# Softmax on negated scores, two scalings of probabilities in place of four, later weight splits and an earlier read of gate sums in a two-layer decoder trunk

## The chip, the core and the metric

The kernel runs on one core of a Trainium2 chip. The core has five engines with a queue each, which work side by side and wait for one another by semaphores: TensorE (PE, with PEld for its weight loads), VectorE (DVE), ScalarE (ACT), GpSimd (POOL) and SyncE (SP), which here only issues DMAs. ACT issues a few DMAs too. The metric is the time of one execution on the device, in microseconds.

## What is computed

A trunk of two layers over 256 tokens of width 1024, all in float32. A layer is a half step of SwiGLU, a mixer, and another half step of SwiGLU; one RMS norm closes the trunk.

```python
for l in range(DEPTH):                     # 2
    x = x + 0.5 * swiglu(rms_norm(x, norm_ffn1[l]), w_ffn1_gate[l], w_ffn1_up[l], w_ffn1_down[l])
    x = x + hybrid_mixer(rms_norm(x, norm_mix[l]), ...)
    x = x + 0.5 * swiglu(rms_norm(x, norm_ffn2[l]), w_ffn2_gate[l], w_ffn2_up[l], w_ffn2_down[l])
return rms_norm(x, norm_final)

def swiglu(x, w_gate, w_up, w_down):       # d_ff 2816
    return (jax.nn.silu(x @ w_gate) * (x @ w_up)) @ w_down

def masked_softmax(s, valid):
    s = jnp.where(valid, s.astype(jnp.float32), NEG)
    m = jnp.max(s, axis=-1, keepdims=True)
    p = jnp.where(valid, jnp.exp(s - m), 0.0)
    return p / jnp.maximum(jnp.sum(p, axis=-1, keepdims=True), 1.0)
```

The mixer projects to queries, keys, values and gates and has 8 NSA heads in two groups (three branches: compressed keys, selected blocks, window) and 8 MoBA heads. At 256 tokens the selected blocks, the window and the MoBA block each cover all earlier tokens, so each head's scores are two blocks of 128 queries against 128 or 256 keys, masked causally. The NSA branches are weighted by gates, and a product with `w_out` closes the mixer.

## The kernel before

**Precision and splits.** Every weight block (128 x 1024, 512 KB, 322 of them in a fixed list) comes by a DMA on SP into one of 5 raw buffers. ACT rounds it to a high part (`whi`, L260), DVE subtracts to get a low part (`wlo`, L290), and TensorE multiplies high by high, high by low and low by high. There are 7 buffer pairs for split blocks. A block is split when a pair is free; `pump` keeps `st.reserve` pairs free, so a larger reserve means later splits. A raw buffer comes free, and the next load starts, when its low part is made.

**Half steps** (`ffn`). In turn of j (22 blocks of 128 hidden units) TensorE makes a gate and an up product (`wide`, L594 and L596: 512 columns with the high part, 256 with the low one, eight times) into PSUM banks: psB and psB for even j, psC and psD for odd. `read(j)` adds the two halves of a bank: ACT copies one (L680), DVE adds the other (L681). Then POOL, ACT and DVE form silu(gate) x up (`finish`), and `down` multiplies it into four banks psA. Where a half step starts behind another stage, its first two j run together (`gu_two`): four blocks, with the last part of the normed input still on its way. The next gate block needs the psB bank back, and so the sums of j = 0.

**Mixer.** `feature_one` makes each feature block with 24 matmuls (L565 to L567); between them stand the attention steps of earlier blocks: scores (`nsa_s`, L1101 and L1103), softmax, `normalize` (scaling by 1/sum and gate, on POOL), `transpose_p` (three transposes a half into a psA bank, L1074, copied out by ACT, L1076), products with the values (`pv`, L1084 and L1086, then the compressed branch, L1123). A softmax of an NSA head has two halves, r = 0 and 1 (selected and window branch); that of a MoBA head has one. For each half DVE adds the mask to the scores, multiplies by `rs8` (1/8 times the norm) and keeps the maximum (L1046 for the 256-wide block, L1047 for the 128-wide one); one instruction negates the maxima (L1049), and ACT makes the exponentials with that bias (L1051, L1052). New queries and keys pass `rope_begin` (ACT copies them raw, L820, and issues two DMAs that swap rows, L821 and L822) and `rope_end` (two POOL products, L826 and L827), then `stack_q` (casts on ACT, L834 and L835, and DVE, L836 and L837). Then come the MoBA values (`m_v`, L1181 to L1183) and the output product (L572 to L574, in `steps`), with the MoBA heads' steps in between.

**Order.** The program names each instruction's engine; the order on each engine is made by a scheduler that runs a model of the engines over the whole program. `tc.issue_after(i)` makes it place an instruction behind i. The stream of splits uses this by `st.behind`: what stands there for "A" or "V" is the instruction behind which ACT's or DVE's part of the following splits must come. The order is fixed when the program is built; on the chip every engine works through its own list.

```python
def queue(self, eng):
    return self.tc.issue_after(self.behind[eng]) if eng in self.behind else nullcontext()
```

Of the kernel before, what the change touches and what calls it, by code (L numbers as in the profile page):

```python
# [21 lines left out]
F32 = mybir.dt.float32  # L22
# [3 lines left out]
AF = mybir.ActivationFunctionType  # L26
OP = mybir.AluOpType
AX = mybir.AxisListType

D, S, L, DH = 1024, 256, 2, 64  # L30
# [287 lines left out]
def trunk(ctx, tc, xin, wst, w1st, gains, glast, cst, small, out, phases=PHASES, n_raw=5, n_hl=7):  # L318
    nc = tc.nc
    V, A, G, T = nc.vector, nc.scalar, nc.gpsimd, nc.tensor  # L320
# [3 lines left out]
    mp = ctx.enter_context(tc.tile_pool(name="mix", bufs=1))  # L324
# [319 lines left out]
    def ffn(pi, name, l):  # L644
# [31 lines left out]
        def read(j):  # L676

            s = S_[j] = mp.tile([128, 2, S], F32, name="hs", tag="PT", bufs=5)
            for i, o in enumerate(pend.pop(j)):
                A.copy(s[:, i], o[:, S:])  # L680
                V.tensor_add(s[:, i], s[:, i], o[:, :S])  # L681

        def finish(j):
            n = 0 if j == NJ - 1 else 1
# [119 lines left out]
    def mixer(pi, l):  # L804
# [95 lines left out]
        rotk = rawk[:, 2:4]  # L900
        rs = state["rs"]
        rs8 = mp.tile([128, 2], F32, name="rs8", bufs=2)
        nrs = mp.tile([128, 2], F32, name="nrs", bufs=2)
        G.tensor_scalar(rs8, rs, DH ** -0.5, None, op0=OP.mult)
        A.activation(warm, rs8[:, 0:1], AF.Exp, scale=0.0)
        G.tensor_scalar(nrs, rs, -1.0, None, op0=OP.mult)
# [130 lines left out]

        def softmax(key, s1, s0, nb, gates):

            P = mp.tile([128, 3, 2, 128], F32, name="P", tag="P", bufs=3)[:, :, :nb]  # L1040
            m = mp.tile([128, 2, nb], F32, name=f"mx{nb}", bufs=3)
            nm = mp.tile([128, 2, nb], F32, name=f"nm{nb}", bufs=3)
            sm = mp.tile([128, 2, nb], F32, name=f"sm{nb}", bufs=3)
            mk = m1.rearrange("p (k t) -> p k t", k=2)
            for r in range(nb):
                V.tensor_tensor_reduce(P[:, 0:2, r], s1[:, :, r], mk, rs8[:, 1:2], -3e38, OP.add, OP.max, m[:, 0, r:r + 1])  # L1046
                read = V.tensor_tensor_reduce(P[:, 2, r], s0[:, r], m0, rs8[:, 0:1], -3e38, OP.add, OP.max,  # L1047
                                              m[:, 1, r:r + 1]).ins
            V.tensor_scalar(nm, m, -1.0, None, op0=OP.mult)  # L1049
            for r in range(nb):  # L1050
                A.activation(P[:, 0:2, r], P[:, 0:2, r], AF.Exp, bias=nm[:, 0, r:r + 1], accum_out=sm[:, 0, r:r + 1])  # L1051
                e = A.activation(P[:, 2, r], P[:, 2, r], AF.Exp, bias=nm[:, 1, r:r + 1], accum_out=sm[:, 1, r:r + 1]).ins  # L1052
            if gates is not None:
                st.behind["A"] = e
            PR[key] = (P, sm, nb, gates)
            return read

        def normalize(key):
            P, sm, nb, gates = PR[key]
            V.reciprocal(sm, sm)  # L1060
            if gates is None:
                V.tensor_scalar(sm, sm, 1.0, None, op0=OP.min)
            else:
                V.scalar_tensor_tensor(sm, sm, 1.0, gates, op0=OP.min, op1=OP.mult)
            for r in range(nb):
                G.tensor_mul(P[:, 0:2, r], P[:, 0:2, r], sm[:, 0, r:r + 1, None].to_broadcast([128, 2, 128]))
                G.tensor_mul(P[:, 2, r], P[:, 2, r], sm[:, 1, r:r + 1].to_broadcast([128, 128]))

        def transpose_p(key, tag):
            P, _, nb, _ = PR.pop(key)  # L1070
# [167 lines left out]
        normalize(5)  # L1238
        m_end()
        nsa_s(6)  # L1240
        st.reserve = 2
        m_feat("mq", 2)
        nsa_pv(1)
        nsa_t(4)
# [62 lines left out]
        nsa_t(6)  # L1307
        normalize(("m", 0))
        moba_s(1)
        st.reserve = 1  # L1310
        st.behind.clear()
        m_v(1)
        nsa_t(7)
# [12 lines left out]
                 (moba_s, 7), (part, 3, 0), (normalize, ("m", 6)), (moba_pv, 2), (part, 3, 1), (moba_t, 6), (part, 4, 0),  # L1326
                 (normalize, ("m", 7)), (moba_t, 7), (part, 4, 1), (moba_pv, 3)]
        for f, *args in steps:
            if args == [4, 0]:
                st.reserve = 0  # L1330
            with tc.issue_after(last):
                last = f(*args) or last
        st.reserve = 1
# [71 lines left out]
```

## Time and profile before

| | before |
|---|---|
| median of 3 runs, us | 1021.62 (1019.35 to 1098.41) |
| profiled execution: its own time, us | 1018.07 |
| its span, first to last instruction, us | 1016.3 |
| busy, us: PE / PEld / DVE / ACT / POOL | 996.7 / 861.8 / 698.2 / 592.6 / 323.0 |
| mean granted TensorE clock | 0.997 |
| read from memory, MB | 182.04 |

About 1.8 us of the profiled execution's time lie outside its span. The stages of the span, in us: half step 0 to 200, first mixer 200 to 330, half steps 330 to 700, second mixer 700 to 830, last half step to the end. A wait is shown as the idle time of an engine ahead of an instruction, with what ended it. Only idle time on the engine that bounds the kernel costs time by itself. An engine's queue of DMA issues is named ACTq or SPq.

### The profile page before, as it was taken

The page shows a single profiled execution, that of the slowest core. Times are in us where ns is not written, and L with a number is a line of the kernel's source. Part 1 is how long each engine was busy: PE and PEld are TensorE (multiplying, and loading weights), DVE is VectorE, ACT ScalarE, POOL GpSimd, SP SyncE. Part 2 cuts the span into 40 slices and gives each one's busy share as a digit, 9 for nine tenths or more (in the row PEclk, how much of TensorE's full clock was granted, in tenths as well). Part 3 has the DMA queues.
Part 4 walks back from the last instruction along what each step waited for, and adds up shares of the span by engine and source line. Part 5 has one row for each costly group of instructions (what it writes and reads, how often), then busy time and mean ns, then how long its engine had stood idle before and what let it go on. Part 6 is the DMA issues. An engine that isn't in the chain of part 4 may idle for free.

```text
span 1016.3 us, 16192 instructions
## 1 busy us (share of the span) xinstructions
PE 996.7 (98%) x5873; PEld 861.8 (85%) x5873; DVE 698.2 (69%) x1195; ACT 592.6 (58%) x1137; POOL 323.0 (32%) x412
## 2 busy tenths in 40 slices
PE   9999999999899999999999999999999999999997
PEld 7888888899778888888888888889987788888885
DVE  6876566689984866666676656666899757666664
ACT  6755555557864855555575555456578756555552
POOL 2322122136751322222242222131477313222220
PEclk9999999999999999999999999999999999999999
DMA  8786776354452666666557677863436427666631
GB/s 275 249 292 198 266 251 214 105 171 149 130 166 84 213 205 193 195 188 189 164 186 207 188 232 231 280 189 125 158 110 185 132 84 252 198 212 187 189 123 42
DMA packets 52848, 188.21 MB, mean 185 GB/s; under 512 B 6368, under 2 KB 6752, under 8 KB 51616
## 3 DMA queue, kind: packets, MB, share of 16 engines
q1 hardware_dynamic: 49680, 182.17, 56.5%
q10 hardware_dynamic: 3088, 5.01, 1.8%
q8 instruction: 46, 0.75, 0.3%
q14 instruction: 34, 0.28, 0.1%
HBM read 182.04 MB, written 1.05 MB: 180 GB/s over the span
## 4 chain that ended last, share of the span: by engine, by line
PE 91%; DVE 4%; ACT 2%; issue 1%; POOL 1%; DMA 1%; ACTq 0%; POOLq 0%; DVEq 0%
PE psB L594 16%; PE psA L572 9%; PE psA L574 9%; PE psA L573 9%; PE psB L596 8%; PE psC L594 8%; PE psD L594 8%; PE psD L596 4%; PE psC L596 4%; PE psA L565 2%; PE psA L566 2%; PE psA L567 2%; PE psA L407 1%; PE psD L1084 1%; DVE wlo L290 1%
## 5 line engine op out<-in xcount | busy, mean ns | idle before, releaser
L290 DVE TENSOR_TENSOR wlo<-wraw,whi 128x1024 fp32r<-128x1024 f32 x325 | 411.1, 1272 | 208.7 <-ACT whi L260 208.3
L260 ACT CAST whi<-wraw 128x1024 fp32r<-128x1024 f32 (+1 forms) x326 | 337.7, 1044 | 276.3 <-issue 172.1
L594 PE MATMUL psB<-x,whi 128*128 128x512 f32 x688 | 242.4, 393 | 1.1 <-DVE hs L681 1.1
L689 POOL TENSOR_TENSOR hs<-hs,rbc 128x256 f32<-128x256 f32 x88 | 76.5, 871 | 400.7 <-DVE hs L681 366.5
L596 PE MATMUL psB<-x,wlo 128*128 128x256 f32 x688 | 192.6, 280 | 0.0
L594 PEld LDWEIGHTS psB<-x,whi 128*128 128x128 f32 x688 | 129.2, 188 | 30.0 <-DVE hs L681 1.9
L574 PE MATMUL psA<-wlo,hp 128*128 128x512 f32 (+1 forms) x356 | 137.6, 387 | 0.0
L573 PE MATMUL psA<-whi,hp 128*128 128x512 f32 (+1 forms) x356 | 137.5, 387 | 0.0
L572 PE MATMUL psA<-whi,hp 128*128 128x512 f32 (+1 forms) x356 | 137.0, 388 | 0.5 <-DVE X L470 0.5
L596 PEld LDWEIGHTS psB<-x,wlo 128*128 128x128 f32 x688 | 129.4, 188 | 1.4
L691 POOL TENSOR_TENSOR hs<-hs,rbc 128x256 f32<-128x256 f32 x88 | 101.8, 1160 | 72.2 <-ACT hs L690 72.0
L594 PE MATMUL psC<-x,whi 128*128 128x512 f32 x344 | 122.0, 392 | 0.0
L594 PE MATMUL psD<-x,whi 128*128 128x512 f32 x344 | 121.7, 391 | 0.0
L596 PE MATMUL psC<-x,wlo 128*128 128x256 f32 x344 | 96.2, 280 | 0.0
L596 PE MATMUL psD<-x,wlo 128*128 128x256 f32 x344 | 96.2, 280 | 0.0
L572 PEld LDWEIGHTS psA<-whi,hp 128*128 128x128 f32 x356 | 66.8, 188 | 14.3 <-DVE X L470 0.7
L574 PEld LDWEIGHTS psA<-wlo,hp 128*128 128x128 f32 x356 | 66.8, 188 | 13.7
L573 PEld LDWEIGHTS psA<-whi,hp 128*128 128x128 f32 x356 | 66.9, 188 | 12.2
L594 PEld LDWEIGHTS psD<-x,whi 128*128 128x128 f32 x344 | 64.6, 188 | 14.3
L594 PEld LDWEIGHTS psC<-x,whi 128*128 128x128 f32 x344 | 64.6, 188 | 14.1
L565 PE MATMUL psA<-x,whi 128*128 128x256 f32 x256 | 73.0, 285 | 0.0
L567 PE MATMUL psA<-x,wlo 128*128 128x256 f32 x256 | 72.3, 282 | 0.0
(245 smaller groups left out, 1599.8 us busy)
## 6 DMA issues: line engine op xcount, KB each, us to landing
wraw<-in_w SPq DMA_DIRECT2D x318, 512.0 KB, 4.3
W1a<-in_w SPq DMA_DIRECT2D x4, 1024.0 KB, 6.2
W1mixn<-in_w SPq DMA_DIRECT2D x2, 1024.0 KB, 6.4
W1late<-in_w SPq DMA_DIRECT2D x2, 1024.0 KB, 5.9
KM<-KM ACTq DMA_DIRECT2D x8, 256.0 KB, 3.8
wraw<-in_w SPq DMA_DIRECT2D x4, 420.0 KB, 3.1
wraw<-in_w SPq DMA_DIRECT2D x4, 256.0 KB, 4.8
X<-in_small SPq DMA_DIRECT2D x1, 1024.0 KB, 7.3
```

The source lines that it names most:

```text
L260: self.last_hi = self.nc.scalar.copy(hi[:, a:b], raw[:, a:b]).ins
L290: eng.tensor_sub(lo[:, :c], raw[:, :c], hi[:, :c].bitcast(F32))
L565: T.matmul(o, hi, xh, start=first, stop=False, skip_group_check=True)
L566: T.matmul(o, hi, xl, start=False, stop=False, skip_group_check=True)
L567: return T.matmul(o, lo, xh, start=False, stop=last, skip_group_check=True).ins
L572: T.matmul(o, parts[:, 0, c], hi, start=first, stop=False, skip_group_check=True)
L573: T.matmul(o, parts[:, 1, c], hi, start=False, stop=False, skip_group_check=True)
L574: return T.matmul(o, parts[:, 0, c], lo, start=False, stop=last, skip_group_check=True).ins
L594: T.matmul(o, blk128(hi, k), x.rearrange("p a t -> p (a t)"), start=k == 0, stop=k == KT - 1, skip_group_check=True)
L596: last = T.matmul(o[:, S:], blk128(lo, k), x[:, 0], start=False, stop=k == KT - 1, skip_group_check=True).ins
L689: G.tensor_mul(g, g, state["rbc"])
L691: G.tensor_mul(g, g, state["rbc5"])
```

## The change

Four things are changed.

1. Softmax: DVE multiplies scores plus mask by a negated factor (`nrs8`, a new tile of two values made on POOL) and keeps the minimum, which is the negated maximum. The instruction that negated is gone; ACT's exponentials take `scale=-1.0`.
2. `normalize`: one scaling for the 128-wide blocks of all halves, then one for the 256-wide ones, in place of two for each half.
3. `st.reserve` stays at 3 through the second part of the attention and the MoBA values. It goes to 2, 1 and 0 in the output product, ahead of its blocks 0, 2 and 4.
4. In `read(0)` of a half step other than the first, the second of DVE's two adds is put in `st.behind["V"]`: low parts of blocks that are split from then on come behind it on DVE.

```diff
             for i, o in enumerate(pend.pop(j)):
                 A.copy(s[:, i], o[:, S:])
-                V.tensor_add(s[:, i], s[:, i], o[:, :S])
+                add = V.tensor_add(s[:, i], s[:, i], o[:, :S]).ins
+            if j == 0 and pi > 0:
+                st.behind["V"] = add
...
+        nrs8 = mp.tile([128, 2], F32, name="nrs8", bufs=2)
         nrs = mp.tile([128, 2], F32, name="nrs", bufs=2)
+        G.tensor_scalar(nrs8, rs, -DH ** -0.5, None, op0=OP.mult)
...
-            m = mp.tile([128, 2, nb], F32, name=f"mx{nb}", bufs=3)
...
             for r in range(nb):
-                V.tensor_tensor_reduce(P[:, 0:2, r], s1[:, :, r], mk, rs8[:, 1:2], -3e38, OP.add, OP.max, m[:, 0, r:r + 1])
-                read = V.tensor_tensor_reduce(P[:, 2, r], s0[:, r], m0, rs8[:, 0:1], -3e38, OP.add, OP.max,
-                                              m[:, 1, r:r + 1]).ins
-            V.tensor_scalar(nm, m, -1.0, None, op0=OP.mult)
+                V.tensor_tensor_reduce(P[:, 0:2, r], s1[:, :, r], mk, nrs8[:, 1:2], 3e38, OP.add, OP.min,
+                                       nm[:, 0, r:r + 1])
+                read = V.tensor_tensor_reduce(P[:, 2, r], s0[:, r], m0, nrs8[:, 0:1], 3e38, OP.add, OP.min,
+                                              nm[:, 1, r:r + 1]).ins
             for r in range(nb):
-                A.activation(P[:, 0:2, r], P[:, 0:2, r], AF.Exp, bias=nm[:, 0, r:r + 1], accum_out=sm[:, 0, r:r + 1])
-                e = A.activation(P[:, 2, r], P[:, 2, r], AF.Exp, bias=nm[:, 1, r:r + 1], accum_out=sm[:, 1, r:r + 1]).ins
+                A.activation(P[:, 0:2, r], P[:, 0:2, r], AF.Exp, scale=-1.0, bias=nm[:, 0, r:r + 1],
+                             accum_out=sm[:, 0, r:r + 1])
+                e = A.activation(P[:, 2, r], P[:, 2, r], AF.Exp, scale=-1.0, bias=nm[:, 1, r:r + 1],
+                                 accum_out=sm[:, 1, r:r + 1]).ins
...
-            for r in range(nb):
-                G.tensor_mul(P[:, 0:2, r], P[:, 0:2, r], sm[:, 0, r:r + 1, None].to_broadcast([128, 2, 128]))
-                G.tensor_mul(P[:, 2, r], P[:, 2, r], sm[:, 1, r:r + 1].to_broadcast([128, 128]))
+            G.tensor_mul(P[:, 2], P[:, 2], sm[:, 1, :, None].to_broadcast([128, nb, 128]))
+            G.tensor_mul(P[:, 0:2], P[:, 0:2], sm[:, None, 0, :, None].to_broadcast([128, 2, nb, 128]))
...
         nsa_s(6)
-        st.reserve = 2
         m_feat("mq", 2)
...
         moba_s(1)
-        st.reserve = 1
         st.behind.clear()
...
-            if args == [4, 0]:
-                st.reserve = 0
+            if f is part and args[0] in (0, 2, 4) and args[1] == 0:
+                st.reserve = 2 - args[0] // 2
```

The scheduler makes a new order of the mixers and of the starts of the half steps from this. Three places follow. Line numbers of the rows after the change are those of the changed program, a few higher.

**DVE, start of the second half step of layer 1.** `x` is the normed input's low part, `wlo` a block's low part, `hs` a gate or up sum. Before:

```order
L389 SCALAR_TENSOR_TENSOR x_3575<-psA,g,x_3575 128x256 x4
L290 TENSOR_TENSOR wlo<-wraw,whi 128x1024 x4
L681 TENSOR_TENSOR hs<-hs,psB 128x256
L290 TENSOR_TENSOR wlo<-wraw,whi 128x1024
L681 TENSOR_TENSOR hs<-hs,psB 128x256
L681 TENSOR_TENSOR hs<-hs,psC 128x256
```

and after:

```order
L389 SCALAR_TENSOR_TENSOR x_3529<-psA,g,x_3529 128x256 x4
L681 TENSOR_TENSOR hs<-hs,psB 128x256 x2
L290 TENSOR_TENSOR wlo<-wraw,whi 128x1024 x3
L681 TENSOR_TENSOR hs<-hs,psC 128x256
L290 TENSOR_TENSOR wlo<-wraw,whi 128x1024 x2
L681 TENSOR_TENSOR hs<-hs,psD 128x256
```

Both sums of j = 0 now come ahead of all low parts, where four and then one stood ahead of them. The same has happened at the start of both half steps of layer 2. TensorE's list at this place, behind the last block of `gu_two` (psD), is after the change:

```order
L596 MATMUL psD<-x_3529,wlo 128x256
L594 MATMUL psB<-x_3529,whi 128x512 x2
L596 MATMUL psB<-x_3529,wlo 128x256
L594 MATMUL psB<-x_3529,whi 128x512
L596 MATMUL psB<-x_3529,wlo 128x256
```

Before, high and low products alternated from the first on; now one high product of the up block stands ahead of the first low product of the gate block.

**ACT, first mixer, from head 4's exponentials on.** `PcT` and `PT` are transposes copied out of PSUM (the two `PT` are head 2's), `qs` the casts of queries, `mraw` and `SW` a raw copy of new keys and its two DMAs. Before:

```order
L1031 COPY PcT<-psA 128x256
L834 CAST qs<-rotmq 64x256
L835 CAST qs<-rotmq 64x256
L834 CAST qs<-rotmq 64x256
L835 CAST qs<-rotmq 64x256
L1076 COPY PT<-psA 128x384 x2
L820 COPY mraw<-psA 128x512
L1076 COPY PT<-psA 128x384
L1091 CAST mixn<-psD 128x256
L821 DMA SW<-mraw 16x512
L822 DMA SW<-mraw 16x512
```

and after:

```order
L822 COPY mraw<-psA 128x512
L823 DMA SW<-mraw 16x512
L1035 COPY PcT<-psA 128x256
L1081 COPY PT<-psA 128x384 x2
L836 CAST qs<-rotmq 64x256
L837 CAST qs<-rotmq 64x256
L836 CAST qs<-rotmq 64x256
L837 CAST qs<-rotmq 64x256
L824 DMA SW<-mraw 16x512
```

The raw copy, its first DMA and the copies of head 2's transposes have moved ahead of the casts; the second DMA stays behind them.

**POOL, first mixer, heads 3 to 5.** `P` is a head's probabilities (told apart by `sm`: 2672, 2787 and 2845 are heads 3, 4 and 5 before; 2661, 2772 and 2826 after), `SW` and `rotmq` the two products of a rotary step. Before:

```order
L826 TENSOR_TENSOR SW<-SW,const 128x512
L827 TENSOR_TENSOR rotmq<-rotmq,SW 128x512
L1066 TENSOR_TENSOR P<-P,sm_2672 128x2x128
L1067 TENSOR_TENSOR P<-P,sm_2672 128x128
...
L1067 TENSOR_TENSOR P<-P,sm_2787 128x128
L826 TENSOR_TENSOR SW<-SW,SK 128x512
L827 TENSOR_TENSOR rotmq<-rotmq,SW 128x512
L1066 TENSOR_TENSOR P<-P,sm_2845 128x2x128
L1067 TENSOR_TENSOR P<-P,sm_2845 128x128
```

and after:

```order
L828 TENSOR_TENSOR SW<-SW,const 128x512
L1071 TENSOR_TENSOR P<-P,sm_2661 128x256
L1072 TENSOR_TENSOR P<-P,sm_2661 128x512
L829 TENSOR_TENSOR rotmq<-rotmq,SW 128x512
L1071 TENSOR_TENSOR P<-P,sm_2772 128x256
L1072 TENSOR_TENSOR P<-P,sm_2772 128x512
L828 TENSOR_TENSOR SW<-SW,SK 128x512
L829 TENSOR_TENSOR rotmq<-rotmq,SW 128x512
L1071 TENSOR_TENSOR P<-P,sm_2826 128x256
L1072 TENSOR_TENSOR P<-P,sm_2826 128x512
```

Head 3's scalings have moved between the two products of the rotary step; head 5's stand behind both products of the next step, as before. On TensorE, between head 4's and head 5's transposes, the product with the values of heads 2 and 3 (`nsa_pv(1)`) has moved behind head 5's first half, and the rest of the features and most of the first MoBA scores have moved ahead of it.

## Rows read from the trace of the kernel before

**Rows 1.** The page's busy times: share of the span, instructions.

```profile
PE 996.7 (98%) x5873; PEld 861.8 (85%) x5873; DVE 698.2 (69%) x1195; ACT 592.6 (58%) x1137; POOL 323.0 (32%) x412
```

**Rows 2.** Stretches: us, then busy PE, PEld, DVE, ACT, POOL; clock, DMA, GB/s.

```profile
200.00:300.00 100.00, 94.88 (x739) 84.48 (x738) 87.72 (x203) 71.32 (x173) 56.46 (x68) 0.98 0.51 155
300.00:330.00 30.00, 30.00 (x172) 23.73 (x169) 14.63 (x40) 15.61 (x40) 6.74 (x20) 1.00 0.29 89
330.00:350.00 20.00, 19.44 (x116) 16.98 (x115) 17.08 (x24) 16.84 (x29) 7.45 (x10) 1.00 0.62 211
700.00:800.00 100.00, 95.68 (x754) 84.89 (x754) 89.35 (x207) 72.46 (x178) 58.09 (x68) 1.00 0.51 155
800.00:850.00 50.00, 49.45 (x280) 40.76 (x279) 32.11 (x62) 32.71 (x68) 13.20 (x28) 1.00 0.44 142
```

**Rows 3.** Waits of TensorE, whole span: us in total, times, longest.

```profile
PE psA L1074 <- POOL P L1067: 6.1, 7, 2.1
PE psA L1074 <- ACT PT L1076: 2.2, 2, 1.1
PE psB L594 <- DVE hs L681: 1.1, 2, 0.6
```

**Rows 4.** Timeline of TensorE, head 5: start, us, instruction, idle time before it.

```profile
270.63 0.55 PE L1074 MATMUL psA<-const,P 128*128 128x128 f32 x3 [2.15 <-POOL P L1067]
...
272.99 0.55 PE L1074 MATMUL psA<-const,P 128*128 128x128 f32 x3 [1.34 <-POOL P L1067]
```

**Rows 5.** Stretches behind head 5, columns as in rows 2.

```profile
274.00:276.00 2.00, 2.00 (x9) 1.81 (x8) 1.68 (x8) 1.85 (x10) 1.45 (x5) 0.50 0.56 216
276.00:278.00 2.00, 2.00 (x8) 1.53 (x8) 1.40 (x5) 2.00 (x7) 1.11 (x1) 0.74 0.78 176
```

**Rows 6.** Timeline of the first mixer: POOL, ACT and TensorE up to head 5.

```profile
240.48 0.61 POOL L1066 TENSOR_TENSOR P<-P,sm 128x256 f32<-128x256 f32 x1 [0.17 <-DVE sm L1064]
...
258.42 0.86 ACT L1076 COPY PT<-psA 128x384 f32<-128x384 f32 x2
...
260.38 0.60 ACTq L822 DMA_DIRECT2D SW<-mraw  x1
...
265.07 1.28 POOL L826 TENSOR_TENSOR SW<-SW,SK 128x512 f32<-128x512 f32 x1 [4.43 <-DMA SW<-mraw]
...
265.62 0.65 PE L1084 MATMUL psD<-PT,late 128*64 128x256 f32 x4
...
267.42 0.59 PE L1103 MATMUL psC<-KK,qs 128*128 128x256 f32 x2
...
268.55 1.67 POOL L1066 TENSOR_TENSOR P<-P,sm 128x256 f32<-128x256 f32 x1
```

**Rows 7.** Timeline of two starts: layer 1, second half step; layer 2, first.

```profile
333.26 4.63 DVE L290 TENSOR_TENSOR wlo<-wraw,whi 128x1024 fp32r<-128x1024 f32 x4 [0.46 <-ACT whi L260]
...
337.71 0.40 ACT L680 COPY hs<-psB 128x256 f32<-128x256 f32 x1
...
337.81 0.41 DVE L681 TENSOR_TENSOR hs<-hs,psB 128x256 f32<-128x256 f32 x1
...
338.28 0.50 PE L594 MATMUL psB<-x,whi 128*128 128x512 f32 x1 [0.56 <-DVE hs L681]
...
522.08 0.39 ACT L680 COPY hs<-psB 128x256 f32<-128x256 f32 x1
...
522.27 0.39 PE L594 MATMUL psD<-x,whi 128*128 128x512 f32 x1
522.50 0.28 PE L596 MATMUL psD<-x,wlo 128*128 128x256 f32 x1
```

**Rows 8.** Groups by line and shape: count, busy us, mean ns, idle before.

```profile
L1049 DVE TENSOR_SCALAR nm<-mx 128x4 f32<-128x4 f32 x16 | 5.5, 341 | 0.2
...
L1066 POOL TENSOR_TENSOR P<-P,sm 128x256 f32<-128x256 f32 x48 | 43.0, 897 | 33.3 <-DVE sm L1062 23.3 <-PE psC L1074 5.2 <-PE psA L574 4.0
L1067 POOL TENSOR_TENSOR P<-P,sm 128x128 f32<-128x128 f32 x48 | 31.0, 647 | 0.0
```

## Prediction

> **What bounds the kernel now.** I read the page's busy times first. TensorE is busy for 996.7 of 1016.3 us [rows 1]; 19.6 us are idle on it, and the change neither adds nor removes a matmul. The stretches come next [rows 2]: 5.1 us of the idle time lie in the first mixer (200 to 300), 0.56 at the start of the half step behind it, and 4.3 and 0.55 in the same two places of layer 2. That is 10.5; the remaining 9.1 lie at the program's start and end, where nothing is changed. What ended the waits is in the list of TensorE's waits [rows 3]: 6.1 us for the scaling of probabilities on POOL (L1067), 2.2 us for a PSUM bank that ACT had not yet copied out (L1076), and 1.1 us for the first gate sums (L681). The longest place is head 5's pair of transposes in layer 1, with 2.15 and 1.34 us of idle time [rows 4]. Just behind it the granted clock reads 0.50 and 0.74 in two stretches of 2 us in which TensorE is fully busy [rows 5]: it had idled before, fell to its lower level (1.2 GHz), and lost 1.0 + 0.5 = 1.5 us. If all of these went, the execution would take 1018.07 - 10.5 - 1.5 = 1006 us. That floor is 1.2% under today, whatever the other engines save.
>
> **The negated scores.** Each of 32 softmaxes loses one instruction on DVE: 16 of 341 ns [rows 8], and 16 smaller ones for the MoBA heads, so up to 11 us in all. The exponentials of one half no longer wait for the other half's maxima. DVE is busy for 87.7 and 89.4 us of its two stretches of 100 us [rows 2], so this is room and not path: zero by itself, under the matmuls of the features; were DVE the bound, it would give all of it. Two more scalings of 2 elements on POOL lie far ahead of any softmax and cost nothing there; uncovered they are well under 1 us.
>
> **Two scalings in place of four.** By the means [rows 8] a head costs POOL 2 x (0.897 + 0.647) = 3.09 us now. The new pair is a 256-wide one, 0.90 us, and a 512-wide one, which the trace does not have for P; its nearest row is the 512-wide product at L826, 1.28 us [rows 6]. That gives 2.18 us: the second transpose of a head can start 0.9 us earlier, the first one 1.28 - 0.65 = 0.63 us later, since it now needs both instructions. A 256-wide scaling takes 0.61 us at 240.48 and 1.67 us at 268.55 [rows 6], where DVE makes splits beside it. So a scaling loses some 1.06 us when it meets one of them, and with two instructions a head it can lose that twice, not four times.
>
> The Trainium skill (SBUF — State Buffer, section "SBUF: two separate sides") says that a GpSimd instruction that reads SBUF and a DVE instruction with two SBUF inputs share one pair of ports, held for a whole instruction. The two rows just named agree with it. Against the change it says that the wider product holds a split off for longer, which is the fourth rival.
>
> **What the new order makes of the mixers.** Head 3's second transpose waits 1.1 us in each layer for a bank, because ACT copies head 2's transposes out behind four casts of queries. Now these copies stand ahead of the casts. I take 0.3 us as left: -1.6 us in two layers, bounds 0 and -2.2.
>
> Head 5: POOL reaches its scalings at 268.55 because the product ahead (L826) waits until 265.07 for a DMA that ACT issues at 260.38 [rows 6]. In the new order the raw copy and the first of its two DMAs go ahead of the bank copies, but the second DMA still follows the casts, and head 5 still follows both rotary products on POOL. The casts end at 258.42 today, where the copies behind them start [rows 6]. Head 3's scalings (2.2 us) now precede the rotary product that they need, and ACT's other work hides about half of that: 259.5. With the same 4.7 us from issue to start the product begins about 264.2 and head 5 is ready near 268. TensorE came there at 270.63 - 2.15 = 268.5. Now pv(1), 1.8 us from 265.62 to 267.42 [rows 6], is moved behind, four feature matmuls (0.5) and three score matmuls (0.7) are moved ahead, and the bank wait (0.8) is gone: 267.1. So I leave 0.9 us of the 3.49: -2.6 us (bounds 0 and -3.5). Shorter waits should leave the clock alone: -1.5 us (bounds 0 and -1.5). POOL's other waits are 6.1 - 3.5 = 2.6 us, most of them in layer 2: -0.9 us (bounds 0 and -2.6).
>
> Against it, an earlier TensorE meets DVE sooner. The MoBA values need two banks, one of which DVE frees by reading the last raw queries; in the new order that read lies behind two key splits. I put 0.5 us a layer on it (below 0, above the bank wait of today, 1.1): +1.0 us.
>
> **Weights held back.** By the new order DVE makes 13 low parts instead of 14, and ACT 11 high parts instead of 14, between the gates and the MoBA values; the rest moves into the output product. There DVE is busy for 14.6 of 30 us and TensorE never waits [rows 2], so the move costs nothing; uncovered, one low part is 1.2 us. The loads on SP's queue wait for raw buffers and move with the splits. Four weight blocks stay ready, some 11 us of TensorE's work at 8 x (0.23 + 0.12) = 2.8 us each [rows 7].
>
> **Gate sums ahead of splits.** This touches the start of three half steps. Today DVE makes four low parts from 333.26, 4.63 us, and only then, at 337.81, reads the first gate's sums; TensorE waits 0.56 us for that bank [rows 7]. The change removes this wait but queues the low parts of the very next blocks behind both sums. The second sum needs ACT's copy, which ends at 337.71 + 0.40 = 338.11, and ACT's order up to it is the same. So from 333.26 on DVE does little but wait; it finishes the second sum at 338.11 + 0.41 = 338.5 and the first low part at 338.5 + 4.63/4 = 339.66. TensorE is done with the four blocks at 338.28 - 0.56 = 337.72. It can do two high products of 0.23 us and then needs that low part: it idles for 339.66 - 337.72 - 0.46 = 1.5 us where it idled for 0.56, so +0.9. In layer 2's first half step ACT's copy ends at 522.47, and TensorE is done at about 522.62 with no wait today [rows 7]; the low part comes at 524.0, so +0.9 again. Layer 2's second half step is like the first: +0.9. Sum +2.7 us. Bounds: -1.1, if the sums came early enough, and +5.9, if each first low part also loses 1.06 us to a product of POOL. Later blocks are not late: each takes TensorE 2.8 us and DVE 1.2.
>
> **Sum.** 1018.07 - 1.6 - 2.6 - 1.5 - 0.9 + 1.0 + 2.7 = 1015.2, so 1015 us. The runs shown have a median of 1021.62 and a lowest of 1019.35, a little above the profiled execution; a median may read 1 to 3 us above the sum.
>
> **The rivals.**
> First, everything turns out kindly: no wait is left in the mixers, the clock stays up, the sums come early. 1018.07 - 2.2 - 3.5 - 1.5 - 2.6 - 1.1 = 1007 us. For it speaks that each wait is short; against it, that ACT's copies of the sums stay where they were.
> Second, head 5 waits in full: POOL's queue is unchanged just ahead of it, and the clock falls as before. 1015.2 + 2.6 + 1.5 = 1019 us.
> Third, slower: the low parts that queue behind the sums. At their upper bound, with half of the mixers' 6.6 us gained, the time is 1018.07 + 5.9 - 3.3 = 1021 us. It decides from 2.2 us a start, where three starts eat all that the mixers give.
> Fourth, the wide product delays DVE: each of 16 heads holds a split off for 1.28 - 0.61 = 0.67 us longer, 10.7 us in two layers. DVE has 12.3 and 10.6 us of idle time in the two stretches, so most is hidden; with half on the path, the time is 1015.2 + 5.3 = 1020.5 us.
>
> **Chances.** Forecast (1010 to 1018) 0.55; first rival 0.15; second 0.15; third 0.10; fourth 0.05. The range from 1007 to 1021 leaves out some 0.15; the likeliest case alone spans 1010 to 1018. Faster by over 2%, which is about what a measurement of this kernel can tell from no change, means under 998 us and lies below the floor: 0.02. Slower by over 2% needs a term that nothing here shows: 0.03. Within 2%: 0.95.
>
> **What would show it.** In layer 1, TensorE's wait for POOL at head 5 under 1.5 us, with the clock at 1.00 behind it; the bank wait of 1.1 us gone in both layers; at the start of three half steps a wait of some 1.5 us for a low part (L290) in place of that for a gate sum, with DVE idle for about 4 us ahead of it; more splits in the output product, and no wait there. I would be wrong if waits for low parts spread beyond the first block, if the clock fell at a new place, or if the transposes, now four heads' halves in a row, waited for banks.

## The result, and the profile after

The changed kernel takes 1012.55 us (median of 5 runs, 1012.09 to 1013.27) against 1019.35 us (1016.51 to 1098.41); the ratio is 0.9934, 95% interval 0.9912 to 0.9956. The execution of 1098.41 us was in a slower state, 8% above the others, and the ratio leaves it out. The forecast was 1015 us and within 2%. The profiled execution is the one of 1012.55 us, 5.5 us under that of before, where the sum of the prediction had 2.9.

Stretches of the changed kernel, columns as in [rows 2]:

```profile
200.00:300.00 100.00, 98.42 (x771) 87.15 (x770) 87.03 (x207) 74.64 (x188) 53.05 (x57) 1.00 0.53 160
330.00:350.00 20.00, 18.72 (x103) 15.85 (x102) 18.19 (x22) 14.37 (x25) 8.87 (x8) 1.00 0.66 223
...
700.00:800.00 100.00, 98.04 (x765) 86.60 (x763) 86.28 (x205) 73.67 (x187) 53.40 (x54) 1.00 0.53 163
800.00:850.00 50.00, 48.71 (x269) 40.55 (x268) 31.43 (x46) 31.23 (x60) 13.17 (x24) 1.00 0.40 131
```

TensorE's idle time in the mixers fell from 5.12 to 1.58 us and from 4.32 to 1.96 us. At the three starts of half steps it rose: 0.56 to 1.28, 0 to 0.64, 0.55 to 1.29 us. Its waits, columns as in [rows 3]:

```profile
PE psB L596 <- DVE wlo L290: 1.9, 3, 0.6
PE psA L1186 <- DVE rotmq L825: 1.8, 2, 0.9
PE psB L594 <- DVE hs L681: 1.3, 2, 0.7
PE psA L1079 <- POOL P L1072: 1.1, 2, 0.6
...
PE psA L1079 <- POOL P L1071: 0.3, 1, 0.3
```

The waits for ACT's bank copies (2.2 us) are gone, and 1.4 of 6.1 us are left for POOL. New are the low parts (L290) at the starts and a bank that DVE's read of the last raw queries (L825) frees late.

Idle time is not all that a stop costs, so I also compare how long the stages take, from TensorE's first product of each. Before, and after (start, length in us of the instruction):

```profile
193.48 0.28 PE L565 MATMUL psA<-x,whi 128*128 128x256 f32 x1
...
325.11 0.40 PE L594 MATMUL psB<-x,whi 128*128 128x512 f32 x1
...
694.58 0.28 PE L565 MATMUL psA<-x,whi 128*128 128x256 f32 x1
...
824.24 0.40 PE L594 MATMUL psB<-x,whi 128*128 128x512 f32 x1
...
1009.24 0.28 PE L574 MATMUL psA<-wlo,hp 128*128 128x256 f32 x1
```

```profile
193.02 0.28 PE L565 MATMUL psA<-x,whi 128*128 128x256 f32 x1
...
319.21 0.40 PE L594 MATMUL psB<-x,whi 128*128 128x512 f32 x1
...
690.85 0.28 PE L565 MATMUL psA<-x,whi 128*128 128x256 f32 x1
...
817.35 0.40 PE L594 MATMUL psB<-x,whi 128*128 128x512 f32 x1
...
1003.42 0.28 PE L574 MATMUL psA<-wlo,hp 128*128 128x256 f32 x1
```

| stage, us | before | after | difference |
|---|---|---|---|
| up to the first mixer | 193.48 | 193.02 | -0.46 |
| first mixer | 131.63 | 126.19 | -5.44 |
| two half steps | 369.47 | 371.64 | +2.17 |
| second mixer | 129.66 | 126.50 | -3.16 |
| last half step, to the last product | 185.28 | 186.35 | +1.07 |

So the mixers gave 8.6 us, the starts took 3.2 back, and 0.5 at the program's start is no effect of the change: in the other profiles here that stage takes 192.9 to 193.7.

### The profile page after: what moved, and what is told of

Same layout as the page of the kernel before. It is cut to its first block, busy times and chain, and to the rows that moved or that the text cites. A ratio compares the mean times of both kernels' runs of the same rounds, so it can differ in the third digit from the quotient of the medians.

```text
span 1010.5 us, 16093 instructions
## 1 busy us (share of the span) xinstructions
PE 995.4 (99%) x5873; PEld 861.1 (85%) x5873; DVE 695.9 (69%) x1163; ACT 592.3 (59%) x1137; POOL 311.4 (31%) x382
## 4 chain that ended last, share of the span: by engine, by line
PE 94%; DVE 3%; ACT 2%; issue 1%
PE psB L594 15%; PE psA L572 9%; PE psA L574 9%; PE psA L573 9%; PE psB L596 8%; PE psC L594 7%; PE psD L594 7%; PE psC L596 4%; PE psD L596 4%; PE psA L567 3%; PE psA L565 3%; PE psA L566 3%; ACT whi L260 1%; PE psD L1089 1%; PE psA L1079 1%; PE psA L1186 1%
## 5 line engine op out<-in xcount | busy, mean ns | idle before, releaser
L290 DVE TENSOR_TENSOR wlo<-wraw,whi 128x1024 fp32r<-128x1024 f32 x325 | 412.6, 1278 | 191.8 <-ACT whi L260 191.7
L573 PE MATMUL psA<-whi,hp 128*128 128x512 f32 (+1 forms) x356 | 137.5, 387 | 0.0
L572 PE MATMUL psA<-whi,hp 128*128 128x512 f32 (+1 forms) x356 | 134.1, 388 | 0.5 <-DVE X L470 0.5
```

The costliest lines, as they stand in the source:

```text
L290: eng.tensor_sub(lo[:, :c], raw[:, :c], hi[:, :c].bitcast(F32))
L572: T.matmul(o, parts[:, 0, c], hi, start=first, stop=False, skip_group_check=True)
L573: T.matmul(o, parts[:, 1, c], hi, start=False, stop=False, skip_group_check=True)
```

## The experiments

Each is compared with the kernel before on the same chip. There the kernel before had medians of 1018.49 (E1 to E4), 1017.90 (E5 to E8) and 1018.55 us (E9 to E11). "Mixers" are the two stage lengths as in the table.

### The starts of the half steps: E1, E2, E4

E1 is the changed kernel without part 4.

```diff
-                add = V.tensor_add(s[:, i], s[:, i], o[:, :S]).ins
-            if j == 0 and pi > 0:
-                st.behind["V"] = add
+                V.tensor_add(s[:, i], s[:, i], o[:, :S])
```

> The changed kernel with part 4 undone: DVE's sums of the first gate are again not put ahead of the low parts. In the mixers the order on all five engines stays that of the changed kernel; only the three starts of half steps differ. Theory A (low parts queued behind both sums cost time): the idle time of TensorE at the three starts returns from 1.28, 0.64 and 1.29 us to 0.56, 0 and 0.55 us, so 2.1 us less than the changed kernel: about 1010.4 us. Theory B (part 4 earns its keep, and the waits at the starts come from something else, such as the high parts on ACT): the waits stay or the time rises, 1012.5 to 1013.5 us.

Measured: 1009.02 us, ratio 0.9908 (0.9895 to 0.9921). The half steps take 369.51 and 185.28 us, 2.13 and 1.07 less than in the changed kernel. Theory A holds, and its size was too small: 3.2 us by the stages, not 2.1.

E2 is the kernel before with part 4 alone.

```diff
-                V.tensor_add(s[:, i], s[:, i], o[:, :S])
+                add = V.tensor_add(s[:, i], s[:, i], o[:, :S]).ins
+            if j == 0 and pi > 0:
+                st.behind["V"] = add
```

> The kernel before with part 4 alone: the mixers keep their old order, the three starts get the new one. Theory A: the starts lose 0.72 + 0.64 + 0.74 = 2.1 us, so a profiled execution takes 1018.1 + 2.1 = 1020.2 us, with a wait for a low part (L290) of some 0.64 us three times. Theory B (removing the wait for the first gate's sum gains): 1.1 us less than before, 1017.0 us.

Measured: 1021.43 us, ratio 1.0023 (1.0011 to 1.0035). The half steps take 371.63 and 186.33 us, as in the changed kernel. Part 4 costs time by itself, whatever the mixers do.

Why it does is read from the start of the second half step of layer 1 in the changed kernel (start, length, instruction, idle time before it). ACT, DVE, TensorE:

```profile
326.29 2.93 ACT L260 CAST whi<-wraw 128x1024 fp32r<-128x1024 f32 x3
...
330.86 1.07 ACT L260 CAST whi<-wraw 128x1024 fp32r<-128x1024 f32 x1
331.81 0.39 ACT L680 COPY hs<-psB 128x256 f32<-128x256 f32 x1
...
331.01 0.42 DVE L681 TENSOR_TENSOR hs<-hs,psB 128x256 f32<-128x256 f32 x1 [4.11 <-ACT hs L680]
332.23 0.42 DVE L681 TENSOR_TENSOR hs<-hs,psB 128x256 f32<-128x256 f32 x1 [0.80 <-ACT hs L680]
332.57 4.03 DVE L290 TENSOR_TENSOR wlo<-wraw,whi 128x1024 fp32r<-128x1024 f32 x3
...
331.66 0.40 PE L594 MATMUL psB<-x,whi 128*128 128x512 f32 x1
332.71 0.51 PE L594 MATMUL psB<-x,whi 128*128 128x512 f32 x1 [0.65 <-DVE hs L681]
333.84 0.39 PE L596 MATMUL psB<-x,wlo 128*128 128x256 f32 x1 [0.63 <-DVE wlo L290]
```

DVE stands idle for 4.11 us in front of the sums, though three high parts lie ready for it from 329.22 on. The second sum waits for ACT's copy, which runs behind a cast of 1.07 us. Only then do the low parts begin, and TensorE needs the first of them. From 331.66 to 333.84 it starts two products that elsewhere take steps of 0.23 us: 2.18 - 0.46 = 1.72 us are lost, of which 1.28 are shown as idle time. Before, 0.56 us were shown at this place, and 0.72 were lost: the product ahead takes a step of 0.12 us, and the next one starts at 338.28 [rows 7].

```profile
337.44 0.28 PE L596 MATMUL psD<-x,wlo 128*128 128x256 f32 x1
```

E4 keeps part 4 but lets the first three low parts go ahead of the sums.

```diff
         self.behind = {}
+        self.free = {"A": 0, "V": 0}
...
     def queue(self, eng):
+        if self.free[eng]:
+            self.free[eng] -= 1
+            return nullcontext()
...
             if j == 0 and pi > 0:
-                st.behind["V"] = add
+                st.behind.update(V=add)
+                st.free.update(V=3)
```

> The changed kernel with part 4 kept, but the three low parts that are split first may come ahead of the sums; only the later ones come behind them. Theory A (what costs is the first low part, which TensorE needs 0.46 us after it starts on the next gate block, not the wait for the gate sums as such): three low parts ahead of the sums end before the gate's bank is read, and both waits at each start go, 1.28 + 0.64 + 1.29 = 3.2 us less than the changed kernel, about 1009.3 us, below the kernel with part 4 undone. Theory B (the start is bound by ACT, whose second copy of sums stands behind a cast of 1.07 us): the waits of about 0.6 us a start remain, 1011 to 1012 us.

Measured: 1007.65 us, ratio 0.9895 (0.9881 to 0.9908). DVE at the same start:

```profile
327.34 3.50 DVE L294 TENSOR_TENSOR wlo<-wraw,whi 128x1024 fp32r<-128x1024 f32 x3 [0.46 <-ACT whi L264]
330.99 0.42 DVE L685 TENSOR_TENSOR hs<-hs,psB 128x256 f32<-128x256 f32 x1 [0.16 <-ACT hs L684]
332.21 0.42 DVE L685 TENSOR_TENSOR hs<-hs,psB 128x256 f32<-128x256 f32 x1 [0.80 <-ACT hs L684]
```

The three low parts fill what was idle time, the first sum comes as early as in the changed kernel, and TensorE does not wait at any of the three starts. The half steps take 368.69 and 184.50 us: 4.8 us less than in the changed kernel, 1.6 less than with four low parts ahead of the first sum (E1). Theory A holds, with more than the 3.2 us it gave. ACT's second copy comes as late as before, so theory B falls.

### What made the mixers shorter: E5 to E10

E5 to E7 put one part alone into the kernel before; E8 takes part 1 out of the changed kernel. Of part 1, the lines that matter:

```diff
-            V.tensor_scalar(nm, m, -1.0, None, op0=OP.mult)
...
-                A.activation(P[:, 0:2, r], P[:, 0:2, r], AF.Exp, bias=nm[:, 0, r:r + 1], accum_out=sm[:, 0, r:r + 1])
+                A.activation(P[:, 0:2, r], P[:, 0:2, r], AF.Exp, scale=-1.0, bias=nm[:, 0, r:r + 1],
+                             accum_out=sm[:, 0, r:r + 1])
```

> The kernel before with part 1 alone (scores negated on reading, one DVE instruction less in each softmax; four scalings on POOL as before). The order that the scheduler makes of the mixers from this is, on ACT and TensorE up to the MoBA values, that of the changed kernel: bank copies ahead of the casts of queries, the product with the values of heads 2 and 3 behind head 5's first half. Theory E (the new order carries the mixers' gain, and part 1 alone makes it): the two bank waits of 1.1 us and most of head 5's 3.5 us go, the clock stays up, and the two mixers, which took TensorE 131.6 and 129.7 us and take it 126.2 and 126.5 in the changed kernel, come to some 127 to 128 us each: a profiled execution of about 1012 us. Theory F (the gain comes from less work on POOL, that is from part 2): little changes, 1017 us.

Measured: 1014.76 us, ratio 0.9962 (0.9949 to 0.9976); mixers 130.18 and 130.89 us in the profiled execution, which at 1017.63 us was the longest of eight. Theory E is half right: the bank waits and most of head 5's wait are gone, but a new wait has come. TensorE's waits, and DVE and TensorE at that place:

```profile
PE psB L1278 <- DVE nm L1049: 5.3, 2, 2.6
PE psA L1077 <- POOL P L1070: 1.2, 2, 0.6
```

```profile
269.14 2.78 DVE L290 TENSOR_TENSOR wlo<-wraw,whi 128x1024 fp32r<-128x1024 f32 x2
271.84 0.47 DVE L1047 CUSTOM_DVE_ANT_0 P<-psB,const,nrs 128x256 f32<-128x256 f32 x1
...
272.74 1.11 PE L1278 MATMUL psB<-KM,qs 128*128 128x256 f32 x4 [2.63 <-DVE nm L1049]
```

The scores of MoBA head 2, the third (the expectations below call them the second), take the psB bank that head 0's scores fill, as there are two. Head 0's softmax, which frees it, stands on DVE behind two low parts.

E6 is part 2 alone.

```diff
-            for r in range(nb):
-                G.tensor_mul(P[:, 0:2, r], P[:, 0:2, r], sm[:, 0, r:r + 1, None].to_broadcast([128, 2, 128]))
-                G.tensor_mul(P[:, 2, r], P[:, 2, r], sm[:, 1, r:r + 1].to_broadcast([128, 128]))
+            G.tensor_mul(P[:, 2], P[:, 2], sm[:, 1, :, None].to_broadcast([128, nb, 128]))
+            G.tensor_mul(P[:, 0:2], P[:, 0:2], sm[:, None, 0, :, None].to_broadcast([128, 2, nb, 128]))
```

> The kernel before with part 2 alone (two scalings of probabilities a head). The order changes too: ACT still copies head 2's transposes out behind the casts, but POOL makes head 5's scalings ahead of the second rotary product instead of behind it. Theory E: the bank waits stay (1.1 us in each layer); head 5 is ready earlier by the second product (1.45 us) and by 0.77 us a head, so about half of its waits and the clock's fall go: -3 us, 1015 us. Theory F (POOL's work was the bound of the mixers): all waits for POOL go, 6.1 us, and the clock stays up: 1010.5 us.

Measured: 1016.36 us, ratio 0.9990 (0.9978 to 1.0001), mixers 130.26 and 130.07 us. Neither theory hits the size, and the interval does not set the 1 us apart from nothing. The waits for POOL are nearly gone, but waits for ACT have taken their place:

```profile
PE psA L1073 <- ACT PcT L1031: 1.8, 2, 0.9
...
PE psA L1073 <- POOL P L1066: 0.6, 2, 0.4
```

E7 is part 3 alone.

```diff
-        st.reserve = 2
...
-        st.reserve = 1
...
-            if args == [4, 0]:
-                st.reserve = 0
+            if f is part and args[0] in (0, 2, 4) and args[1] == 0:
+                st.reserve = 2 - args[0] // 2
```

> The kernel before with part 3 alone (weights held back until the output product). Up to the MoBA values the order stays as before; fewer high and low parts are made between gates and MoBA values. The prediction costs it at nothing: 1018 us, with no wait for a low part in the output product. Rival: with fewer splits beside them, POOL's scalings at head 5 run faster (0.6 us in place of 1.7 us each) and the wait there shrinks: -2 to -4 us.

Measured: 1015.63 us, ratio 0.9979 (0.9968 to 0.9989), mixers 130.37 and 128.42 us. No low part is waited for in the output product, as predicted; yet the part is not worth nothing. The waits for POOL stay at 5.5 us, so the rival's mechanism is not the main reason. In the mixers TensorE idles for 7.4 us in place of 9.4: 0.9 us less for banks that ACT copies out, 0.5 less for POOL, and a wait of 0.5 us for the bank of MoBA scores is gone. Which of the moved low parts does which was not tested.

E8 is the changed kernel with the hunks of part 1 taken back.

> The changed kernel with part 1 undone: the DVE instruction that negates the maxima is back in each softmax, and ACT again copies head 2's transposes out behind the casts of queries. Theory E: the bank waits of 1.1 us come back in both layers and part of head 5's wait with them, about 4 us more than the changed kernel, 1016.5 us. Theory F: the two scalings keep the gain, within 1 us of the changed kernel, 1012.5 to 1013.5 us.

Measured: 1018.59 us, ratio 1.0006 (0.9994 to 1.0018), mixers 129.66 and 129.50 us. Without part 1 nothing is left of the gain: the mixers are still 2.1 us shorter than before, but part 4 costs its 3.2 us in the half steps (371.63 and 186.33 us). ACT's copies are waited for again, and take the place of the waits for POOL:

```profile
PE psA L572 <- ACT PT L1078: 2.2, 2, 1.1
```

E9 and E10 take part 1 with one other part: the hunks of parts 1 and 3, and those of parts 1 and 2.

> The kernel before with parts 1 and 3, without parts 2 and 4. On TensorE, DVE and ACT the order is that of the changed kernel with part 4 undone (1009.0 us), but for one transpose in each layer; only POOL differs, which scales in four instructions a head again. Theory G (the mixers' gain needs the order from part 1 and the held-back low parts of part 3 together, and part 2 adds little): the mixers take TensorE some 127 us each, with waits for POOL at head 5 that are 0.5 to 0.8 us longer than with two scalings, and no wait for DVE's minima; about 1010 us. Rival H (without the saving on POOL head 5 waits as before): 2 to 4 us of waits for POOL come back in layer 1 alone, 1013 to 1015 us.

Measured: 1010.94 us, ratio 0.9923 (0.9906 to 0.9940), mixers 128.41 and 127.08 us. Rival H falls: the waits for POOL are 1.3 us in the two layers, no more than with two scalings (1.6 in E1). Theory G has the size, but not those longer waits for POOL. What is longer than in E1 are waits for DVE: 1.2 us for a psC bank, which E1 does not have, and this one for the bank of the last raw queries, 1.8 us in E1:

```profile
PE psA L1184 <- DVE rotmq L823: 2.8, 2, 1.4
```

> The kernel before with parts 1 and 2, without parts 3 and 4. TensorE's order puts the second MoBA scores ahead of the MoBA values, as with part 1 alone. Theory G: without part 3 two low parts (2.8 us) stand on DVE ahead of the first MoBA softmax; the second MoBA scores wait some 2.5 us for their bank in each mixer, and the clock falls behind it in some executions: about 1014 us, as with part 1 alone. Rival H (part 2 gives the rest of the gain): 1009 to 1010 us.

Measured: 1013.92 us, ratio 0.9955 (0.9938 to 0.9973), mixers 127.35 and 127.65 us in the profiled execution, which at 1011.56 us was the fastest of eight (granted clock 0.999; the others 0.995 to 0.997). By the median theory G holds. The new wait of E5 is there as expected:

```profile
PE psB L1277 <- DVE nm L1049: 4.2, 2, 2.1
```

| parts in the kernel | us | | parts in the kernel | us |
|---|---|---|---|---|
| none | 1017.9 to 1019.4 | | 1 and 2 | 1013.92 |
| 1 | 1014.76 | | 1 and 3 | 1010.94 |
| 2 | 1016.36 | | 1, 2 and 3 | 1009.02 |
| 3 | 1015.63 | | 2, 3 and 4 | 1018.59 |
| 4 | 1021.43 | | all four | 1012.55 |

Theory G stands. Part 1 brings the order that removes the bank waits and lets head 5 through, and with it the scores of MoBA head 2 meet DVE too early. Part 3 takes one of the two low parts from in front of head 0's softmax, and in TensorE's list the scores of head 2 then stand behind 18 of the products of the MoBA values; the two come together, and make some 4 us on top of part 1. Part 2 is worth 1.5 us (by the ratios, whose intervals overlap) to 1.9 us (by the medians) on top of both: from E9 to E1, where TensorE's list differs at one transpose in each layer, and the computing instructions of DVE and ACT stand in the same order.

### The bank ahead of the MoBA values: E3, E11

E3 puts a low part behind DVE's read of the last raw queries in the changed kernel.

```diff
-            V.tensor_mul(ro, src, ctab[:, None, :].to_broadcast([128, 2, S]))
+            return V.tensor_mul(ro, src, ctab[:, None, :].to_broadcast([128, 2, S])).ins
...
-                rope_begin(cur["b"], raw, sw, ro, tabs[0])
+                freed = rope_begin(cur["b"], raw, sw, ro, tabs[0])
+                if (which, i) == ("mq", 3):
+                    st.behind["V"] = freed
```

> The changed kernel; in the mixers one low part of weights is put behind DVE's read of the last raw queries (L825) instead of ahead of it, by one line that sets the instruction behind which splits come. Theory C (TensorE's wait of 0.92 us for a bank, ahead of the MoBA values, in each mixer comes from what stands ahead of that read in DVE's queue, and the low part is 1.23 us of it): both waits go, 1.8 us less than the changed kernel, about 1010.7 us. Rival D (the read itself is late because the raw queries or DVE's other work are late): the wait stays within 0.3 us of 0.92, about 1012.5 us.

Measured: 1012.63 us, ratio 0.9941 (0.9928 to 0.9954): a miss for theory C. The wait is the same 0.92 us. DVE and TensorE show why:

```profile
269.24 0.48 DVE L1050 CUSTOM_DVE_ANT_0 P<-psB,const,nrs 128x256 f32<-128x256 f32 x1 [1.11 <-PE psA L1079]
...
269.65 0.69 DVE L825 TENSOR_TENSOR rotmq<-psA,const 128x512 f32<-128x512 f32 x1
...
265.33 0.36 PE L1281 MATMUL psB<-KM,qs 128*128 128x256 f32 x1
...
268.71 0.38 PE L1079 MATMUL psA<-const,P 128*128 128x128 f32 x2
...
270.48 0.47 PE L1188 MATMUL psA<-whi,x 128*128 128x512 f32 x1 [0.92 <-DVE rotmq L825]
```

With the low part gone, DVE idles for 1.11 us instead. In its list the read stands behind the first MoBA softmax (L1050). That softmax's scores were complete at 265.69, but the trace puts its wait down to head 5's last transposes (L1079, to 269.09). This fits the program: `P` has three buffers, and the softmax of MoBA head 0, three after head 5's, takes the buffer that those transposes read. TensorE waits for a read that is queued behind something that waits for TensorE. But rival D is not right either: the raw queries were not late, as the read follows the softmax without a wait.

E11 starts from E4 and puts that softmax, too, behind the read (with the hunk of E3, where `freed` is kept in `cur`).

```diff
-            softmax(("m", h), s[:, :S].rearrange("p (b r t) -> p b r t", b=2, r=1),
-                    s[:, S:S + 128].rearrange("p (r t) -> p r t", r=1), 1, None)
+            with tc.issue_after(cur["freed"]):
+                softmax(("m", h), s[:, :S].rearrange("p (b r t) -> p b r t", b=2, r=1),
+                        s[:, S:S + 128].rearrange("p (r t) -> p r t", r=1), 1, None)
```

> The kernel with three low parts ahead of the gate sums (1007.65 us), and in the mixers DVE's read of the last raw queries now ahead of the first MoBA softmax as well as of the low part. Theory C2 (TensorE's wait of 0.92 us ahead of the MoBA values comes from that softmax in DVE's queue: its scores are made only just before, so a read queued behind it is late whatever else is moved): DVE is free for the read some 1.5 us earlier, both waits go, and with the pace lost at each stop the time falls by 2.0 to 2.4 us, to about 1005.5 us. Rival D (the raw queries are late): the waits stay, 1007.5 us.

Measured: 1005.21 us (1004.79 to 1006.60), ratio 0.9868 (0.9849 to 0.9887). DVE's read starts at 267.79, and TensorE goes on without a wait. So theory C2 had the right neighbour; its reason, scores made only just before, is not what E3's trace shows.

```profile
267.79 0.69 DVE L830 TENSOR_TENSOR rotmq<-psA,const 128x512 f32<-128x512 f32 x1
...
269.16 0.42 PE L1193 MATMUL psA<-whi,x 128*128 128x512 f32 x1
```

No part of the computation is left out of this kernel, and it is faster than both: 7.3 us under the changed kernel, 13.3 under the one before.

## Why the prediction was right, and where it was not

**The sum.** 1015.2 was forecast, 1012.55 measured, inside the range of the likeliest case; but the gain was forecast at about half its size. In idle time and clock, the terms were:

| term | forecast, us | shown, us |
|---|---|---|
| bank copies, both layers | -1.6 | -2.2 |
| head 5, layer 1 | -2.6 | -2.9 |
| clock | -1.5 | -1.5 |
| POOL's other waits | -0.9 | -1.8 |
| MoBA values' bank | +1.0 | +1.8 |
| starts of half steps | +2.7 | +2.1 |
| not forecast: waits of 1.0 us for MoBA scores and values late in layer 2 gone, 0.2 us new | 0 | -0.8 |

That makes -5.3 where -2.9 was forecast; with the 0.5 us at the program's start it is the whole of the -5.5, but for some tenths. That the terms close so well is luck: by the stages the mixers gave 8.6 us, where the terms hold 7.4, and the starts took 3.2, where they hold 2.1, and these two shortfalls cancel.

**Mixers: right in kind, and the step to head 5 was wrong.** TensorE and POOL there, after:

```profile
265.78 0.55 PE L1079 MATMUL psA<-const,P 128*128 128x128 f32 x3 [0.55 <-POOL P L1072]
```

```profile
257.65 1.89 POOL L828 TENSOR_TENSOR SW<-SW,SK 128x512 f32<-128x512 f32 x1 [1.62 <-DMA SW<-mraw]
...
263.29 1.44 POOL L1071 TENSOR_TENSOR P<-P,sm 128x256 f32<-128x256 f32 x1 [2.31 <-DVE sm L1070]
264.69 1.03 POOL L1072 TENSOR_TENSOR P<-P,sm 128x512 f32<-128x512 f32 x1
```

Of the 3.49 us, 0.55 are left where 0.9 were forecast. But the chain that led to 0.9 put the rotary product at 264.2, because "the second DMA still follows the casts" (it does in the list, but not in time, see the last section). The product starts at 257.65, and POOL then idles for 2.31 us until the softmax hands over its sums: head 5 now waits for DVE and ACT, not for the rotary step. TensorE came some 2.3 us earlier than forecast as well, so that two errors left the difference nearly right, by luck. The clock read 1.00 in all stretches behind head 5, against 0.50 and 0.74 [rows 5].

**Which part does it.** The prediction priced the new order without saying which part makes it, and set the negated scores themselves to zero. E5 and E8 show that the mixers' gain hangs on this part, by the order that comes with it: 3 us alone, and 6 us with the others (E8 against the changed kernel). What the saved instructions are worth as busy time on DVE, with the old order, no run shows. Weights held back were also set to nothing, since the low parts find cover in the output product. That is so, but what they leave behind was overlooked: one low part in front of a DVE softmax that TensorE waits for (E5, E9, E10).

**MoBA values' bank.** The step "that read lies behind two key splits" named the wrong neighbour, so that 0.5 us a layer was taken where 0.92 came. E3 and E11 show the right one: a softmax that waits for TensorE itself, by E3's trace for head 5's last transposes.

**Starts.** The mechanism was forecast, with DVE idle for about 4 us (4.11) and a low part late behind the second sum. In two of three starts the sum itself is still waited for, since ACT's second copy is late; the prediction had dropped that wait. It was mis-sized in one more way: idle time shown (2.1) was taken for time lost (3.2 by the stages, 2.3 to 3.5 by E1 and E2). No wait for a low part spread beyond the first block of a start.

**Two scalings.** Forecast 2.18 us a head; the groups after read 1045 + 1276 ns = 2.32 us, so 0.77 are saved against [rows 8], not 0.9.

```profile
L1072 POOL TENSOR_TENSOR P<-P,sm 128x512 f32<-128x512 f32 x16 | 20.4, 1276 | 0.0
...
L1071 POOL TENSOR_TENSOR P<-P,sm 128x256 f32<-128x256 f32 x16 | 16.7, 1045 | 12.3 <-DVE sm L1070 9.1 <-DVE sm L1066 2.6 <-ACT whi L260 0.3
```

The fourth rival, that the wide product holds DVE off, is not borne out. With equal lists on DVE, a low part takes as long beside two scalings (E1, the first fence) as beside four (E9):

```profile
L290 DVE TENSOR_TENSOR wlo<-wraw,whi 128x1024 fp32r<-128x1024 f32 x319 | 404.7, 1276 | 205.1 <-ACT whi L260 204.9
```

```profile
L290 DVE TENSOR_TENSOR wlo<-wraw,whi 128x1024 fp32r<-128x1024 f32 x319 | 403.7, 1272 | 205.6 <-ACT whi L260 205.3
```

The third rival had the right place and the wrong size: 1.1 us a start, half of the 2.2 from which it decides.

## What to carry to other kernels

An edit that frees an engine that isn't the bound can still be worth the most, through the order that a scheduler makes of it: price the order, and part by part, since here part 1 alone brought a wait that only part 3 took away. When a wait is moved ahead on a queue, ask what else the engine could have done meanwhile, and leave that work in front (E4); when a read that frees a bank is late, look at every neighbour ahead of it for one that waits for the engine that waits (E11).

## What the runs showed of the hardware that was not expected

**A DMA issue can run ahead of computing instructions that precede it in its engine's list.** In ACT's list after the change, the second DMA (L824) stands behind the four casts; in the trace it starts 0.73 us before the first of them:

```profile
255.82 0.49 ACTq L824 DMA_DIRECT2D SW<-mraw  x1
...
256.55 0.41 ACT L836 CAST qs<-rotmq 64x256 fp32r<-64x256 f32 x1
```

Nothing in it needs the casts, and it did not wait for them. The Trainium skill (Perfetto Trace Analysis, section "Sequencer Loop") says that an engine's sequencer reads instruction after instruction, pushes engine instructions into a queue, where they wait for semaphores, and starts control instructions itself. The trace agrees, if a DMA issue counts among the latter, which that section does not say. It is this that the step to head 5 had left out. The product that needs the DMA follows 1.8 us later, where 4.7 us lay between before the change [rows 6]; why this is shorter was not tested.

**A stop costs TensorE more than its idle time.** Two stops with 1.28 us of idle time cost 1.72 us at the start above. The 1.72 goes by starts alone; how it divides into idle and busy time is rougher, since the profile models where a product ends.

**The clock makes a part of the spread.** In 31 executions of the kernel before (those beside E5 to E8), the time runs from 1014.67 us at a mean granted clock of 0.999 to 1021.01 at 0.993. The changed kernel, whose waits in the mixers are all under 1 us, kept 0.998 to 0.999 and a spread of 1.2 us. The profiled execution of before, at 0.997, had one fall, of 1.5 us. That of E2 (0.995), whose mixers have the order of before, had two, one in each layer, of some 1.7 us each; a stretch of the second:

```profile
752.00:754.00 2.00, 2.00 (x11) 2.00 (x11) 1.76 (x5) 1.54 (x7) 1.88 (x4) 0.50 0.58 223
```

The clock does not explain all: of the 17 executions beside E1 to E4, one took 1017.17 us at 0.994 and another 1020.34 at 0.996. The change seems to take away this loss too, which one profile can price too low; five executions of the changed kernel are few to tell. Their median did not end 1 to 3 us above the profiled execution, as the prediction allowed for, but on it.
